# A two-layer hybrid DiT kernel: ScalarE's copies of the chunk inverses issued later, a seventh early spare block, and a third product bank in layer two

## The chip, the cores and the metric

One core of one Trainium2 chip runs the whole program. The metric is the device time of one execution in microseconds. The core has a matrix engine (PE, TensorE), a vector engine (DVE), a scalar engine (ACT), GpSimd (POOL) and a queue for transfers (SP); each issues its own instructions in the order in which the program gives them, and waits for the others by semaphores.

## What is computed

Two layers over 512 tokens of width 1024 with 256 context tokens beside them (768 columns in all; the second layer needs the context only as keys, values and starting states). Each layer projects the modulated, normalised input to three branches and to merge logits:

```python
h = rms_norm(x, norm_w[layer]) * (1.0 + scale) + shift
(a_qkv, a_z, a_beta, a_alpha, b_q, b_kv, b_z, c_qkv, c_z, merge) = split(h @ w_in[layer])
o_a = bidir_delta(conv+silu of a_qkv, ...)      # needs inv(L + I) of each 64x64 chunk
y_b = window_attention(q_b, k_b, v_b, k_ctx, v_ctx, sink) * silu(b_z)
o_c = bidir_retention(...)
merged = g_a * (y_a @ w_br[0]) + g_b * (y_b @ w_br[1]) + g_c * (y_c @ w_br[2])
x = x + gate * (merged @ w_o)
```

In branch A (gated delta rule) each chunk of 64 tokens needs the inverse of a unit lower-triangular matrix (`triangular_solve`), for four heads and two directions; queries, keys and values go through a five-tap convolution first. `g_a`, `g_b`, `g_c` are sigmoids of the merge logits, the gates `z` go through silu.

## The kernel before

Activations are kept transposed, 128 features by up to 768 tokens. A projection of one block of 128 outputs (`proj`, L322) takes float32 weights apart into a rounded high part `wh` (a copy on ACT, L306 through the helper L287) and a low part `wl` (four subtractions on POOL, L296), and the activations are held in the same two parts `hh` and `hl`. So one block is 24 matmuls of 512 columns on PE (`prod`, L311, all recorded at L261): 16 with `wh`, then 8 with `wl`. Where context is wanted, 24 more of 256 columns follow. The products go to PSUM tiles: `px` has two banks, `pc` one, `pg` five that serve everything else. The weight tiles `wr`, `wh` and `wl` have two buffers each.

Each layer first projects the blocks of branch A: `ak`, `aq` and `av` of each head. In `delta_proj` the result is convolved: ACT takes the first tap from `px` and `pc` (`t<-px,vec`, `t<-pc,vec`), DVE the other four taps (L290, `t<-px,vec,t` and `t<-pc,vec,t`), ACT applies a tanh, DVE a last L290 on the 768 columns, and PE turns the tile by transposes (L612, written to `pg`).

The inverses go through `delta_inv`: DVE solves the 32x32 corners lane by lane (31 steps, L293), then two stream transposes (L757, L758) bring the result back. It is then scattered to three sets of tiles: `W` by DVE (16 copies, L773), `T` and `Q` by ACT (12 copies of 32x192, L775; in the trace `t<-t 32x192` on ACT). `levels` builds the 64x64 inverses from these with many 32x32 matmuls (L801). `levels` is started by `burst`, which puts its first matmul in the PE order behind a given spare block.

A spare block is a projection whose result is needed only much later: the gates and merge logits, produced by the generator `aside` (L1224 on). Its product is evacuated by ACT with a tanh to a tile `kept` and stored to DRAM. Spare blocks are strewn between other work to keep PE busy; how many go where is the table `FILL` (L36), one row per layer: five numbers for the five weaves of branch A, one for each attention chunk, and one taken right before the token projection `w1` at the end of the attention. `aside` records for each spare block a triple in `self.asides`: the last matmul, an ACT instruction and the end. While `self.behind` is set (the first weave), each spare block is issued after the one before it. The first weave interleaves three generators by their counts:

```python
weave((seq(self.delta_mats(l, last, st[0]), self.delta_inv(st[0], BACK[l][0])), 45),
      (self.delta_proj(l, 1, vec, last, st[1]), 6), fill(F[0]))
```

The order in which the framework puts instructions on each engine follows from this program order, from priorities, and from `issue_after`, which orders one instruction behind another without a semaphore wait.

In the merge (end of `layer`), each of 24 products of 12 matmuls (`y` against `w_br`) goes to a `px` bank, and DVE multiplies it into the kept logits (L290, `t<-t,px`). The first of them run while DVE still normalises the last retention head (`c_norm`, L973 to L981).

Of the kernel before, what the change touches and what calls it, by code (L numbers as in the profile page):

```python
# [9 lines left out]
F32 = mybir.dt.float32  # L10
F32R = mybir.dt.float32r
BF16 = mybir.dt.bfloat16
AF = mybir.ActivationFunctionType
# [19 lines left out]
C1 = 3  # L33
AH = 2
BG = (0, 2)
FILL = ((5, 2, 4, 7, 6, 1, 0), (6, 2, 4, 9, 6, 1, 1))  # L36
BACK = ((2, 3), (2, 2))

NAMES = (["aq%d" % i for i in range(4)] + ["ak%d" % i for i in range(4)]
# [123 lines left out]
class Builder:  # L163
# [135 lines left out]
    def weight(self, dram, kb=KB):  # L299
        nc = self.nc  # L300
        w = self.wr.tile([128, KB, 128], F32, name="wr")[:, 0:kb]
        hi = self.wh.tile([128, KB, 128], F32R, name="wh")[:, 0:kb]
        lo = self.wl.tile([128, KB, 128], F32R, name="wl")[:, 0:kb]
        with self.tc.high_priority(offset=WHI):
            self.fetch = nc.sync.dma_start(w, dram).ins
            self.act(hi, w, AF.Copy)  # L306
            for k in range(0, kb, 2):
                self.gtt(lo[:, k:k + 2], w[:, k:k + 2], hi[:, k:k + 2].bitcast(F32), ALU.subtract)
        return [hi[:, k] for k in range(kb)], [lo[:, k] for k in range(kb)]
# [11 lines left out]

    def proj(self, dram, acts, ctx, w=None, other=False):  # L322
        w = w or self.weight(dram, len(acts))
        px = self.gps() if other else self.px.tile([128, 512], F32, name="px")
        self.prod(px, w, acts, slice(0, SEQ))
        pc = None
        if ctx:
            pc = self.gps(CTX) if other else self.pc.tile([128, 512], F32, name="pc")[:, 0:CTX]
            self.prod(pc, w, acts, slice(SEQ, TOK))
        return px, pc  # L330
# [396 lines left out]
    def delta_inv(self, st, back):  # L727
# [21 lines left out]
        for m in range(31):  # L749
            n, w = 31 - m, m + 1  # L750
# [14 lines left out]
        for d in range(2):  # L765
# [3 lines left out]
            for hh, h in enumerate(st.heads):  # L769
                W[h, d] = self.alloc()  # L770
                nc.gpsimd.memset(W[h, d].f, 0.0)
                for q in range(4):
                    made.append(nc.vector.tensor_copy(blk(W[h, d], q), lane(wsrc, q, d, hh)))  # L773
                for q, t, c in ((own, Q, 32 * (own % 2)), (own + 1 - 2 * d, Q, 32 * (1 - own % 2)), (other, T, 0)):
                    with self.tc.issue_after(self.asides[-back][1]):  # L775
                        made.append(self.act(six(t.f)[32 * q:32 * q + 32, hh, :, c:c + 32],
                                             lane(tsrc, q, d, hh), AF.Copy))
                yield
# [445 lines left out]
    def aside(self, l, last):  # L1224
# [5 lines left out]
        a, b = FILL[l][0], sum(FILL[l][0:4]) - 2  # L1230
        for nm in ms[0:a] + z("a")[0:2] + ms[a:b] + z("a")[2:4] + z("b") + z("c") + ms[b:]:
            px, pc = self.pblk(l, nm, not last, None, self.behind)
            pe = self.last
            t = self.fp.tile([128, TOK], F32, name="kept")
            for ps, sl in ((px, slice(0, SEQ)), (pc, slice(SEQ, TOK)))[:1 if last else 2]:
                th = self.act(t[:, sl], ps, AF.Tanh, scale=0.5)
                if nm[1] == "z":
                    self.stt(t[:, sl], t[:, sl], 1.0, ps, ALU.add, ALU.mult)
            self.asides.append((pe, th.ins, self.end))
            g = self.dp.tile([128, n], F32, name="%s_%d" % (nm, l))  # L1240
            nc.scalar.dma_start(g, t[:, 0:n])
            self.kept[nm] = g
# [10 lines left out]
    def layer(self, l, xs, rs, mod, vec, row, ada):  # L1253
# [9 lines left out]
        for k in range(KB):  # L1263
            self.tap("hh%d_%d" % (l, k), self.hs[k][0].f)
            self.tap("hl%d_%d" % (l, k), self.hs[k][1].f)
        self.asides, self.behind = [], False
        self.fill = self.aside(l, last)
        self.mods = self.ada(ada) if ada else iter(())
        F = FILL[l]
# [38 lines left out]
        for _ in p0:  # L1308
            pass
        self.behind = True  # L1310
        weave((seq(self.delta_mats(l, last, st[0]), self.delta_inv(st[0], BACK[l][0])), 45),
              (self.delta_proj(l, 1, vec, last, st[1]), 6), fill(F[0]))
        self.behind = False
        weave((self.hi(self.delta_chain(l, last, st[0])), 6), fill(F[1]))
        weave((self.hi(self.delta_mats(l, last, st[1])), 4), fill(F[2]))
# [195 lines left out]
```

## Time and profile before

| what | us |
|---|---|
| three executions | 1800.25, 1798.98, 1794.04 |
| median of them | 1798.98 |
| the profiled execution | 1798.01 |
| its span, first to last instruction | 1796.2 |
| PE busy in it | 1703.9 |
| mean granted TensorE clock | 0.982 |

The span is the time from the first to the last instruction of the profiled execution; 1.8 us lie around it. Times in the views are counted from the span's start. In a row of a timeline the first number is the start, the second the duration, `xN` the number of like instructions in a run, and the bracket the idle time of the engine before it with the instruction that ended it. Lines L261, L287, L290, L293 and L296 are those of small helpers (matmul, activation, the two vector operations and the POOL one), so the tile names tell which work it is.

### The profile page before, as it was taken

What the parts mean: (1) busy time and instruction counts of PE and PEld (TensorE: products, weight loads), DVE (VectorE), ACT (ScalarE), POOL (GpSimd) and SP (SyncE); (2) the same over time, 40 slices, a digit from 0 to 9 for tenths busy, and PEclk for the clock granted to TensorE, in tenths of its full rate; (3) what the DMA queues carried; (4) which work ended last, traced back from release to release, by engine and by line L of the source; (5) the groups of instructions that cost most, each with busy time, mean ns of one, the idle gap of its engine ahead of it and who ended that gap; (6) DMA issues with size and microseconds to landing.
All of it is one profiled execution on the core that took longest, in us unless ns stands there. A gap on an engine that the chain in (4) does not pass through costs nothing. (4 is left out here: it accounts for less than half of the span.)

```text
span 1796.2 us, 30682 instructions
## 1 busy us (share of the span) xinstructions
PE 1703.9 (95%) x11574; PEld 1449.5 (81%) x11574; DVE 1062.3 (59%) x2531; ACT 844.8 (47%) x2018; POOL 593.4 (33%) x739
## 2 busy tenths in 40 slices
PE   7899989999999999999999899969999999999997
PEld 4788879889877778988888687859878777888786
DVE  4668758634565464346573657966954667445663
ACT  6565546253454455233133556455554655433244
POOL 2422422412321313121454524433523323322453
PEclk9999999999999999999999999989999999999998
DMA  9202211313234234013444211211423432212552
GB/s 313 82 30 71 86 34 63 112 54 130 103 124 154 91 120 148 24 36 121 147 150 160 83 36 68 86 42 54 148 82 131 138 102 71 89 47 67 164 173 90
DMA packets 73748, 180.67 MB, mean 101 GB/s; under 512 B 8832, under 2 KB 16384, under 8 KB 73600
## 3 DMA queue, kind: packets, MB, share of 16 engines
q1 hardware_dynamic: 62144, 154.07, 26.3%
q10 hardware_dynamic: 11456, 24.65, 3.6%
q8 instruction: 91, 1.49, 0.3%
q14 instruction: 57, 0.47, 0.1%
HBM read 150.89 MB, written 27.79 MB: 99 GB/s over the span
## 5 line engine op out<-in xcount | busy, mean ns | idle before, releaser
L296 POOL TENSOR_TENSOR wl<-wr,wh 128x256 fp32r<-128x256 f32 x640 | 506.6, 821 | 1016.6 <-ACT wh L287 773.6
L261 PE MATMUL px<-hh,wh 128*128 128x512 f32 (+1 forms) x1000 | 392.9, 397 | 13.2 <-ACT wh L287 10.3
L261 PE MATMUL px<-hl,wh 128*128 128x512 f32 (+1 forms) x1000 | 392.3, 395 | 3.9 <-DVE hl L290 2.4
L293 DVE TENSOR_TENSOR t<-t,t 128x512 f32<-128x512 f32 (+21 forms) x411 | 264.3, 644 | 41.0 <-ACT t L287 28.5
L287 ACT ACTIVATE wh<-wr 128x1024 fp32r<-128x1024 f32 (+1 forms) x184 | 174.3, 947 | 220.9 <-PE pc L261 83.1
L261 PE MATMUL px<-hh,wl 128*128 128x512 f32 (+1 forms) x1000 | 262.1, 391 | 0.0
L287 ACT ACTIVATE t<-t 32x192 f32<-32x192 f32 (+10 forms) x314 | 167.4, 546 | 186.7 <-DVE t L290 144.9
L261 PE MATMUL pg<-t,t 128*128 128x128 f32 (+2 forms) x1616 | 230.9, 285 | 11.0 <-DVE t L293 10.6
L261 PEld LDWEIGHTS pg<-t,t 128*128 128x128 f32 x1616 | 205.8, 191 | 33.4 <-issue 11.2
L261 PEld LDWEIGHTS px<-hh,wh 128*128 128x128 f32 x1000 | 190.8, 191 | 52.0 <-ACT wh L287 11.2
L261 PEld LDWEIGHTS px<-hl,wh 128*128 128x128 f32 x1000 | 190.7, 191 | 40.4 <-DVE hl L290 5.7
L261 PEld LDWEIGHTS px<-hh,wl 128*128 128x128 f32 x1000 | 180.7, 189 | 33.2 <-issue 1.2
L261 PE MATMUL pc<-hl,wh 128*128 128x256 f32 x528 | 133.7, 288 | 0.9 <-DVE hl L290 0.8
L261 PE MATMUL pc<-hh,wh 128*128 128x256 f32 x528 | 133.4, 287 | 0.2 <-ACT hh L287 0.2
L287 ACT ACTIVATE t<-pg 128x128 f32<-128x128 f32 (+4 forms) x216 | 77.8, 384 | 108.9 <-PE pg L418 39.7
L261 PE MATMUL px<-t,wh 128*128 128x512 f32 x384 | 100.9, 400 | 4.5 <-DVE t L290 4.2
L261 PEld LDWEIGHTS pc<-hl,wh 128*128 128x128 f32 x528 | 101.2, 192 | 4.7 <-DVE hl L290 1.5
L261 PEld LDWEIGHTS pc<-hh,wh 128*128 128x128 f32 x528 | 101.1, 192 | 4.2 <-issue 1.2
L287 ACT ACTIVATE t<-px 128x128 f32<-128x128 f32 (+2 forms) x120 | 54.6, 465 | 91.2 <-PE px L261 85.3
L261 PE MATMUL px<-t,hh 128*128 128x272 f32 (+1 forms) x384 | 87.5, 316 | 0.3 <-DVE t L290 0.3
L261 PEld LDWEIGHTS px<-t,wh 128*128 128x128 f32 x384 | 71.2, 191 | 19.1 <-DVE t L290 3.1
L261 PE MATMUL pg<-hh,wh 128*128 128x256 f32 (+1 forms) x264 | 79.7, 326 | 3.0 <-DVE t L290 2.9
(192 smaller groups left out, 2657.3 us busy)
## 6 DMA issues: line engine op xcount, KB each, us to landing
wr<-wblk SPq DMA_DIRECT2D x120, 512.0 KB, 3.3
t<-wada SPq DMA_DIRECT2D x48, 384.0 KB, 4.6
wr<-wbr SPq DMA_DIRECT2D x48, 256.0 KB, 2.7
m<-kept ACTq DMA_DIRECT2D x24, 384.0 KB, 2.3
t<-m SPq DMA_DIRECT2D x24, 384.0 KB, 3.4
wr<-wout SPq DMA_DIRECT2D x16, 512.0 KB, 3.5
t<-wada SPq DMA_DIRECT2D x24, 256.0 KB, 4.8
m<-kept ACTq DMA_DIRECT2D x24, 256.0 KB, 2.0
```

The source lines that it names most:

```text
L261: return self.nc.tensor.matmul(out, lhsT=lhsT, rhs=rhs, start=start, stop=stop)
L287: return self.nc.scalar.activation(out, in_, func, **k)
L293: self.nc.vector.tensor_tensor(out=out, in0=in0, in1=in1, op=op)
L296: self.nc.gpsimd.tensor_tensor(out=out, in0=in0, in1=in1, op=op)
```

## The change

Three edits. In `delta_inv` the 12 ACT copies of `T` and `Q` are issued after the last spare block's ACT weight conversion (`self.high`, the copy to `wh`) instead of after the tanh of the spare block two or three back. In `FILL` layer two's first weave takes 7 spare blocks for 6 and none is left for the place before `w1`, and the first weave's count for `delta_proj` is 7 for 6 in both layers. In `proj` every third product of layer two that has no context part and isn't sent to `pg` uses the `pc` bank. After the change the lines from L321 on stand 3 or 4 lines lower (L612 is L615, L758 is L761, L801 is L804).

```diff
-FILL = ((5, 2, 4, 7, 6, 1, 0), (6, 2, 4, 9, 6, 1, 1))
+FILL = ((5, 2, 4, 7, 6, 1, 0), (7, 2, 4, 9, 6, 1, 0))
...
-            self.act(hi, w, AF.Copy)
+            self.high = self.act(hi, w, AF.Copy).ins
...
     def proj(self, dram, acts, ctx, w=None, other=False):
         w = w or self.weight(dram, len(acts))
-        px = self.gps() if other else self.px.tile([128, 512], F32, name="px")
+        self.turns += not (other or ctx)
+        third = self.three and not ctx and self.turns % 3 == 0
+        px = self.gps() if other else (self.pc if third else self.px).tile(
+            [128, 512], F32, name="pc" if third else "px")
...
-                    with self.tc.issue_after(self.asides[-back][1]):
+                    with self.tc.issue_after(self.asides[-1][1]):
...
-            pe = self.last
+            pe, high = self.last, self.high
...
-            self.asides.append((pe, th.ins, self.end))
+            self.asides.append((pe, high, self.end))
...
+        self.three, self.turns = last, 0
...
-              (self.delta_proj(l, 1, vec, last, st[1]), 6), fill(F[0]))
+              (self.delta_proj(l, 1, vec, last, st[1]), 7), fill(F[0]))
```

What moves on the engines, at three places.

PE in layer two's first weave, from the transposes of the last query head (`t608`) to the first matmul of `levels` (L801, L804). `t613` is the convolved last value head, `px_12384`, `pg_12084`, `pg_12074` and `pg_12124` are spare blocks. Before:

```order
L612 MATMUL pg_12030<-c0_108,t608_11856 128x128 x4
L261 MATMUL px_12384<-hh0_85,wh_12376 128x512
...
L261 MATMUL px_12384<-hh4_93,wl_12377 128x512
L612 MATMUL pg_12055<-c0_108,t613_11970 128x128 x4
L612 MATMUL pg_12061<-c0_108,t613_11970 128x128 x2
L261 MATMUL pg_12084<-hh0_85,wh_12076 128x512
...
L801 MATMUL pg_12155<-t619_12116,t572_11203 32x32
```

After:

```order
L615 MATMUL pg_12020<-c0_108,t608_11846 128x128 x4
L615 MATMUL pg_12045<-c0_108,t613_11960 128x128 x4
L615 MATMUL pg_12051<-c0_108,t613_11960 128x128 x2
L261 MATMUL pg_12074<-hh0_85,wh_12066 128x512
...
L261 MATMUL pg_12074<-hh7_99,wl_12067 128x512
L261 MATMUL pg_12124<-hh0_85,wh_12116 128x512
L804 MATMUL pg_12193<-t619_12154,t572_11203 32x32
```

The value head's transposes now stand right behind the query head's; before, 21 matmuls of a spare block stood between. Behind them stand 24 matmuls of one spare block and one of the next, where four matmuls stood; `levels` begins at the same place in the order.

ACT in layer one's first weave, the copies of `T` and `Q` (`32x6x32`), the first taps of the last value head (`t160`) and the conversion `wh_2624` of a spare block. Before:

```order
L287 ACTIVATE t163_2354<-t134_1540 32x6x32 x2
L287 ACTIVATE t163_2354<-t133_1539 32x6x32 x2
L287 ACTIVATE t156_2160<-t155_2149 128x768
...
L287 ACTIVATE wh_2624<-wr_2623 128x1024
...
L287 ACTIVATE t164_2355<-t134_1540 32x6x32 x4
L287 ACTIVATE t164_2355<-t133_1539 32x6x32 x4
L287 ACTIVATE t160_2317<-px_2251,vec0_163 128x512
L287 ACTIVATE wh_2837<-wr_2836 128x1024
L287 ACTIVATE t160_2317<-pc_2276,vec0_163 128x256
```

After:

```order
L287 ACTIVATE r2_2268<-r2_2268 128x12
...
L287 ACTIVATE t164_2355<-t134_1540 32x6x32 x2
L287 ACTIVATE t163_2354<-t134_1540 32x6x32
L287 ACTIVATE t164_2355<-t134_1540 32x6x32 x2
...
L287 ACTIVATE t164_2355<-t133_1539 32x6x32 x2
L287 ACTIVATE t163_2354<-t133_1539 32x6x32
L287 ACTIVATE t160_2243<-px_2177,vec0_163 128x512
L287 ACTIVATE wh_2624<-wr_2623 128x1024
L287 ACTIVATE t160_2243<-pc_2202,vec0_163 128x256
```

The twelve copies were in two lots of four and eight, the first of them ahead of the tanh of `t156` and of `wh_2624`; now all twelve stand in a row, ahead of the first tap of `t160` and of `wh_2624`. On PE the spare block that stood between the projections of the last key and the last query head (`ak3`, `aq3`; 48 matmuls, in `pg`) is gone from there, and `aq3` follows `ak3` at once; 25 matmuls of a spare block in `pg` now stand behind the value head's transposes.

DVE in layer two's merge: products of the merge (`px_16962` on) taken from their banks, between the steps of `c_norm` (L973 to L981 before, L976 to L984 after). Before:

```order
L290 SCALAR_TENSOR_TENSOR t872_16953<-t872_16953,px_16962 128x512
L974 BN_AGGR cmv_16869<-cst_16868 128x2
L290 SCALAR_TENSOR_TENSOR t873_16976<-t873_16976,px_16985 128x512
L981 TENSOR_SCALAR t831_16279<-t831_16279,cmv_16869,crs_16870 128x128 x4
...
L290 SCALAR_TENSOR_TENSOR t868_16921<-pg_16923,nw1_10485,t868_16921 128x512
...
L290 SCALAR_TENSOR_TENSOR t871_16945<-pg_16947,nw1_10485,t871_16945 128x512
L290 SCALAR_TENSOR_TENSOR t874_16999<-t874_16999,px_17008 128x512
L290 SCALAR_TENSOR_TENSOR t875_17022<-t875_17022,px_17031 128x512
```

After:

```order
L290 SCALAR_TENSOR_TENSOR t872_16953<-t872_16953,pc_16962 128x512
L977 BN_AGGR cmv_16869<-cst_16868 128x2
L290 SCALAR_TENSOR_TENSOR t873_16976<-t873_16976,px_16985 128x512
L290 SCALAR_TENSOR_TENSOR t874_16999<-t874_16999,px_17008 128x512
L984 TENSOR_SCALAR t831_16279<-t831_16279,cmv_16869,crs_16870 128x128 x4
...
L290 SCALAR_TENSOR_TENSOR t868_16921<-pg_16923,nw1_10485,t868_16921 128x512
...
L290 SCALAR_TENSOR_TENSOR t871_16945<-pg_16947,nw1_10485,t871_16945 128x512
L290 SCALAR_TENSOR_TENSOR t875_17022<-t875_17022,pc_17031 128x512
L290 SCALAR_TENSOR_TENSOR t876_17045<-t876_17045,px_17054 128x512
L290 SCALAR_TENSOR_TENSOR t877_17068<-t877_17068,px_17077 128x512
```

The third product (`px_17008`) is now taken ahead of the normalisation and the first (`pc_16962`) and fourth (`pc_17031`) lie in the third bank; on PE the product that alternates with the normalised tiles' transposes (L932) was the fourth and is the fifth.

## Rows read from the trace of the kernel before

**Rows 1.** The page, busy time by engine (share of the span, number of instructions).

```profile
PE 1703.9 (95%) x11574; PEld 1449.5 (81%) x11574; DVE 1062.3 (59%) x2531; ACT 844.8 (47%) x2018; POOL 593.4 (33%) x739
```

**Rows 2.** What PE waited for, whole span: us in total, times, longest us.

```profile
PE px L261 <- ACT wh L287: 10.6, 2, 10.3
...
PE pg L612 <- DVE t L290: 9.8, 5, 4.9
```

**Rows 3.** PE in time order, layer two's first weave: start, duration, [idle before <-releaser].

```profile
1179.23 0.63 PE L612 MATMUL pg<-c,t 128*128 128x128 f32 x4 [1.56 <-DVE t L290]
...
1190.20 0.80 PE L261 MATMUL px<-hh,wh 128*128 128x512 f32 x1 [10.34 <-ACT wh L287]
...
1196.89 0.82 PE L612 MATMUL pg<-c,t 128*128 128x128 f32 x6
...
1198.80 1.02 PE L801 MATMUL pg<-t,t 32*32 32x32 f32 x96 [0.16 <-DVE t L773]
```

**Rows 4.** ACT in time order, same stretch.

```profile
1181.90 3.22 ACT L287 ACTIVATE t<-t 32x192 f32<-32x192 f32 x6 [0.36 <-ACT r L287]
...
1189.10 1.06 ACT L287 ACTIVATE wh<-wr 128x1024 fp32r<-128x1024 f32 x1
...
1194.56 0.85 ACT L287 ACTIVATE t<-t 128x768 f32<-128x768 f32 x1 [3.01 <-DVE t L290]
```

**Rows 5.** DVE in time order, same stretch.

```profile
1181.04 4.47 DVE L773 COPY t<-t 32x192 f32<-32x192 f32 x8
...
1185.86 3.10 DVE L290 SCALAR_TENSOR_TENSOR t<-px,vec,t 128x510 f32<-128x510 f32 x4 [0.35 <-ACT t L287]
...
1190.55 1.00 DVE L290 SCALAR_TENSOR_TENSOR t<-pc,vec,t 128x254 f32<-128x254 f32 x2 [1.59 <-ACT t L287]
...
1195.59 0.96 DVE L290 SCALAR_TENSOR_TENSOR t<-t,t 128x768 f32<-128x768 f32 x1
```

**Rows 6.** Stretches: length, busy us of PE, PEld, DVE, ACT, POOL; clock, DMA.

```profile
1190.10:1193.60 3.50, 3.40 (x8) 2.73 (x9) 1.52 (x4) 1.45 (x10) 3.37 (x5) 0.50 0.00 0
...
1254.00:1316.40 62.40, 59.97 (x264) 49.00 (x262) 58.04 (x107) 33.30 (x69) 34.30 (x44) 1.00 0.41 140
...
1316.40:1321.00 4.60, 4.58 (x195) 3.77 (x199) 0.26 (x1) 2.03 (x3) 2.78 (x4) 0.56 0.18 64
...
1534.40:1548.30 13.90, 12.27 (x88) 9.79 (x86) 10.27 (x29) 10.39 (x31) 8.60 (x10) 1.00 0.51 164
```

**Rows 7.** PE in time order, layer one's first weave.

```profile
222.18 0.82 PE L612 MATMUL pg<-c,t 128*128 128x128 f32 x6
...
232.71 1.54 PE L612 MATMUL pg<-c,t 128*128 128x128 f32 x6 [4.90 <-DVE t L290]
...
235.46 1.50 PE L801 MATMUL pg<-t,t 32*32 32x32 f32 x96
```

**Rows 8.** ACT in time order, same stretch of layer one.

```profile
217.76 4.54 ACT L287 ACTIVATE t<-t 32x192 f32<-32x192 f32 x8 [0.30 <-ACT r L287]
...
222.33 0.69 ACT L287 ACTIVATE t<-px,vec 128x512 f32<-128x512 f32 x1
...
222.91 1.05 ACT L287 ACTIVATE wh<-wr 128x1024 fp32r<-128x1024 f32 x1
```

**Rows 9.** DVE in time order, same stretch of layer one.

```profile
206.02 3.06 DVE L290 SCALAR_TENSOR_TENSOR t<-px,vec,t 128x510 f32<-128x510 f32 x4
...
223.05 3.10 DVE L290 SCALAR_TENSOR_TENSOR t<-px,vec,t 128x510 f32<-128x510 f32 x4 [6.45 <-ACT t L287]
```

**Rows 10.** PE in time order, levels of layer two's second inverse.

```profile
1316.42 1.27 PE L801 MATMUL pg<-t,t 32*32 32x32 f32 x96 [2.45 <-ACT t L287]
```

**Rows 11.** PE in time order, layer two's merge.

```profile
1664.63 3.42 PE L261 MATMUL px<-t,wh 128*128 128x512 f32 x8 [2.75 <-DVE t L290]
...
1675.12 2.06 PE L261 MATMUL px<-t,wh 128*128 128x512 f32 x8 [1.31 <-DVE t L290]
```

**Rows 12.** DVE in time order, layer two's merge.

```profile
1666.58 5.17 DVE L981 TENSOR_SCALAR t<-t,cmv,crs 128x128 f32<-128x128 f32 x16 [1.33 <-ACT crs L287]
```

More of the change, by code (lines that the diff above doesn't have):

```diff
@@ L1232, in aside @@
             px, pc = self.pblk(l, nm, not last, None, self.behind)
-            pe = self.last
+            pe, high = self.last, self.high
             t = self.fp.tile([128, TOK], F32, name="kept")
             for ps, sl in ((px, slice(0, SEQ)), (pc, slice(SEQ, TOK)))[:1 if last else 2]:
-                th = self.act(t[:, sl], ps, AF.Tanh, scale=0.5)
+                self.act(t[:, sl], ps, AF.Tanh, scale=0.5)
                 if nm[1] == "z":
                     self.stt(t[:, sl], t[:, sl], 1.0, ps, ALU.add, ALU.mult)
-            self.asides.append((pe, th.ins, self.end))
+            self.asides.append((pe, high, self.end))
             g = self.dp.tile([128, n], F32, name="%s_%d" % (nm, l))
```

## The prediction

> **What bounds the kernel now.** I read the busy row first: PE works 1703.9 us of 1796.2, so the time is PE's work plus PE's holes, and no edit here removes a matmul [rows 1]. So I went on to the list of what PE waited for. The edit about `wh` aims at one hole of 10.3 us; transposes (L612) waiting for DVE lose 9.8 us in five holes [rows 2]. Then came the timelines around both, and the stretches with their granted clock. In layer two's first weave the reader is to see PE stop at 1179.9 after four transposes, start again at 1190.20 with the conversion `wh` that ACT began at 1189.10, turn the last value head at 1196.89 and reach `levels` at 1198.80 [rows 3, 4]. A hole costs more than its length: the eight matmuls after this one took 3.40 us at a granted clock of 0.50, the 1.2 GHz level, where one takes 0.227 us at full clock (59.97 us for 264), so 3.40 - 1.8 = 1.6 us more [rows 6]. The sum below is made against the profiled execution, 1798.01 us, 1.0 under the median 1798.98. A measurement of this kernel can tell about 0.3% or 5.4 us from no change.
>
> **Copies and seventh spare block, layer two's first weave.** The wait for `wh` goes: the spare block that waited no longer stands there. But the value head's transposes now come right behind the query head's, and everything that could fill the hole stands behind them. So I work out when they can run, along DVE, whose order stays the same. The second stream transpose ends at 1181.0; eight copies of 4.47 us follow, to 1185.5; four taps on `px` take 3.10, to 1188.6 (before, they began at 1185.86 after waiting 0.35 for ACT's first tap, so little is gained) [rows 5]. The taps on `pc` waited 1.59 us for ACT, which had twelve copies in two lots of 3.22 us and the conversion of 1.06 ahead of its tap [rows 4, 5]; now that tap is early, and the four taps, two small instructions and a copy take about 2.3 us: 1190.9. ACT's tanh is 0.85, with three DVE copies of 1.07 us beside it, and the last vector step 0.96: 1193.0 against 1196.55 before [rows 4, 5]. So PE idles from 1179.9 to 1193.0, 13.1 us instead of 10.34; after it come 0.6 us of transposes and 25 matmuls of 5.7 us plus 1.6 for the clock: `levels` at 1200.9 against 1198.80 [rows 3, 6]. As many matmuls are done by then as before, so this is **+2 us**. Bounds: -1 (transposes ready at 1190) and +4 (the copies on ACT get in front of the tanh, 0.54 us each).
>
> **The same in layer one.** Here 48 matmuls leave the place between `ak3` and `aq3`, so `aq3` has to wait for the single `pc` bank (about 1.8 us, what DVE needs for the four `pc` taps), and the value head's product ends near 215.3 instead of 222.18 [rows 7]. The inverses come later, since `aq3`'s taps (about 5.5 us; the first four take 3.06) now precede the stream transposes that ended at 206.02: 211.5 [rows 9]. The twelve copies follow behind a table load on ACT, from about 213.2; at 4.54/8 = 0.57 us each they end at 220.0. Behind them wait the tap (0.69) and the conversion (1.05) of the spare block that PE wants next: 221.7 [rows 8]. PE has finished its transposes at about 216.1, so it idles 5.6 us. After 21 matmuls, 4.8 us plus 1.6 for the clock, it is 228.1; the value head is ready 9.6 us after its taps begin, as before (223.05 to 232.7): 230.3 [rows 7, 9]. So another 2.2 us, transposes, 25 matmuls: `levels` near 236.5 against 235.46, with 3.4 us less work done (23 matmuls on `pc`, three on `px`). Against this stands the hole of 4.90 us that goes, already in these times. **+4 us**; bounds +1 (the copies begin at 210) and +6 (they begin where the eight did, at 217.76).
>
> **Layer two's second inverse.** `levels` waits 2.45 us for the last ACT copy, and the clock falls to 0.56 for the next 4.6 us [rows 6, 10]. By the order 17 more spare matmuls now stand ahead of it, 17 x 0.227 = 3.9 us, which is more than the hole even with a conversion of 1.05 us ahead of the copies. **-2.5 us**; bounds -3.3 (the clock stays up as well) and 0 (the copies slide along).
>
> **The spare matmuls have to be missing somewhere**: at the end of layer two's attention. `FILL`'s last number drops to 0, and by the order the last chunk has 1.5 matmuls of 512 columns to fill with instead of 21. That chunk took 13.9 us with 12.27 of PE, 10.27 of DVE and 10.39 of ACT [rows 6]. With 19.5 x 0.227 = 4.4 us taken away PE has 7.9, and ACT and DVE set the pace at 10.4 plus about 1.1 of waits between them: 11.5 - 7.9 = 3.6 us of idle instead of 1.6. I take **+2.5**, since the weights of the token projection are then late too; bounds 0 and +4.4 (the chunk keeps its length).
>
> **The third bank.** In the merge PE waits 2.75 us for a `px` bank, runs eight matmuls in 3.42 us after it, and waits 1.31 us for another [rows 11]. Now the third product finds a free bank and DVE takes it ahead of the normalisation; the one that alternates with the transposes is the fifth. What is late next: the 16 steps at L981, which ACT releases at 1666.58 and which end at 1671.75 [rows 12]; the last transpose can't run sooner. With five matmuls behind it PE has finished the fifth product at 1673.1. Before, this product began at 1675.12 and took 12 x 0.227 = 2.7: 1677.8. **-4.7**, of which I take -4.4; bounds -5.7 (both holes and the 1.6 us) and 0. The Trainium skill says, on the page "Perfetto Trace Analysis" in the section "Matmuls", that independent matmul groups should rotate through different banks so that the evacuation of one overlaps the next; by that alone the whole 5.7 us would go. The rows put the normalisation in the way of about 1 us of it. Elsewhere in layer two the first copy out of a `px` is mostly ahead of PE: nothing. Layer one's second inverse only has its copies overtake one evacuation, on an engine that isn't the last there: nothing, 0.4 us either way.
>
> **Sum**: +2 + 4 - 2.5 + 2.5 - 4.4 = +1.6, so 1798.0 + 1.6 = **1799.6 us**, no change that can be told.
>
> **Rivals.**
> (a) Faster: the holes that the edits aim at go and the cover is not missed. For it speaks that in layer two PE only needs the value head a little earlier and that in layer one four copies ran right behind the stream transposes, before ACT's eight [rows 8]; against it, that all twelve now stand in one row ahead of a conversion. It would be 0 in both first weaves, -2.5, +1 at the attention, -5.7: -7.2, 1790.8.
> (b) Slower: layer one's conversion behind the twelve copies. If they start where the eight started, at 217.76, the spare block's `wh` is there at 226.3 and PE idles 10 us before it; the value head then is ready at 234.9, and `levels` comes 4.6 us later than I say. With layer two's end at its bound (+4.4) this is 1.6 + 4.6 + 1.9 = +8, 1806. It decides from a start of the copies after about 216. For it speaks that ACT was late with just these copies before [rows 8]; against it, that the evacuations that delayed it now stand elsewhere.
> (c) The bank rule in full: both merge holes vanish, 5.7 us instead of 4.4: 1798.3, still no change. The page named above would have it so.
> (d) The order moves, but other work closes ranks everywhere: 1798.
>
> **How the numbers follow.** Forecast 0.35, (c) 0.10, (d) 0.08: together no change 0.53. (a) 0.22, (b) 0.25, a little more than (a) since each of the two weaves has a new wait in a row. The predicted time is that of the forecast. The range takes in (a) and (b) and leaves about one in ten out on each side: 1791 to 1808.
>
> **What would show it.** Right: in layer two one hole of about 13 us on PE ahead of the L615 transposes, ended by DVE, and none ended by `wh`; in layer one a new hole of about 5 us at 221, ended by the conversion `wh`, and a shorter one ahead of the transposes than 4.90; no hole at the second inverse's `levels`; idle of over 3 us in the last attention chunk; no wait of 2.75 us in the merge, and a wait for L984 in its place. Wrong: a hole in layer two under 9 us, no hole for `wh` in layer one, or merge holes of the same sum as before.

## The result and the profile after

| | median us | from, to |
|---|---|---|
| the kernel before (4 runs on the same chip) | 1799.37 | 1794.04, 1800.25 |
| the changed kernel (4 runs) | 1808.18 | 1807.53, 1810.05 |

The ratio is 1.0051, with a 95% interval of 1.0036 to 1.0066: the change costs about 9 us, where 1799.6 was forecast. The profiled execution of the changed kernel took 1808.64 us, its span is 1806.8, 10.6 more than before. The page's busy row shows that PE has the same number of matmuls as in [rows 1]; 6.8 us of the loss are PE busy for longer, at a mean granted clock of 0.977 for 0.982, the rest are holes.

```profile
PE 1710.7 (95%) x11574; PEld 1455.0 (81%) x11574; DVE 1062.8 (59%) x2531; ACT 845.4 (47%) x2018; POOL 595.6 (33%) x739
```

To see where the 10.6 us arise I counted PE's matmuls in both traces and subtracted the start of the n-th before from that of the n-th after. Inside a place whose order changed this difference means little; behind it, it is what the place cost in this one profile; how far that can be trusted stands in the last section. The forecast's terms stand beside.

| place (difference behind it at matmul) | cost, us | forecast |
|---|---|---|
| start, nothing of the change in it (900) | +1.4 | 0 |
| layer one, first weave (2100) | +2.6 | +4 |
| layer one, second inverse (3300) | +1.9 | 0 |
| layer one's merge (6000) | -0.8 | 0 |
| layer two, first weave (8400) | +5.1 | +2 |
| layer two, second inverse and attention end (10500) | +1.8 | -2.5 + 2.5 |
| retention (10800) | +0.6 | 0 |
| third bank in the merge (11100) | -3.4 | -4.4 |
| tail (end of the span) | +1.4 | 0 |

**Layer two's first weave.** PE in time order, which answers to [rows 3] (start, duration, idle before and what ended it): the hole for `wh` is gone and the one ahead of the value head's transposes is 15.24 us, not the 13.1 of the forecast.

```profile
1185.21 0.63 PE L615 MATMUL pg<-c,t 128*128 128x128 f32 x4 [2.43 <-DVE t L290]
1201.07 1.54 PE L615 MATMUL pg<-c,t 128*128 128x128 f32 x6 [15.24 <-DVE t L290]
...
1210.05 1.02 PE L804 MATMUL pg<-t,t 32*32 32x32 f32 x96
```

DVE in time order there, which answers to [rows 5]. The order is the one forecast and the taps on `px` take their 3.10 us as before, but the eight copies take 6.84 us for 4.47.

```profile
1185.14 1.95 DVE L761 STREAM_TRANSPOSE t<-t 128x1024 f32<-128x1024 f32 x1
1187.01 6.84 DVE L776 COPY t<-t 32x192 f32<-32x192 f32 x8
1193.88 3.10 DVE L290 SCALAR_TENSOR_TENSOR t<-px,vec,t 128x510 f32<-128x510 f32 x4
1196.90 0.99 DVE L290 SCALAR_TENSOR_TENSOR t<-pc,vec,t 128x254 f32<-128x254 f32 x2
```

ACT beside it, which answers to [rows 4]: `wh` is converted at 1188.40, while DVE copies; in the kernel before it was converted after them.

```profile
1188.40 1.05 ACT L287 ACTIVATE wh<-wr 128x1024 fp32r<-128x1024 f32 x1
...
1191.24 3.75 ACT L287 ACTIVATE t<-t 32x192 f32<-32x192 f32 x7
```

POOL, whose four subtractions `wl` are released by `wh`: it is busy from 1187.15 to 1193.74, for nearly as long as DVE copies.

```profile
1187.15 1.02 POOL L737 MEMSET t<- 128x1024 f32 x1 [0.61 <-DVE t L761]
...
1188.31 1.64 POOL L296 TENSOR_TENSOR t<-t,r 128x768 f32<-128x768 f32 x1
1189.92 3.14 POOL L296 TENSOR_TENSOR wl<-wr,wh 128x256 fp32r<-128x256 f32 x4
1193.01 0.73 POOL L774 MEMSET t<- 128x768 f32 x1
```

**Layer one's first weave**, PE, which answers to [rows 7]: the three holes forecast are there, 1.63 us for `pc`, 2.89 for `wh` and 0.82 for the transposes in place of 4.90.

```profile
196.75 0.35 PE L261 MATMUL pc<-hh,wh 128*128 128x256 f32 x1 [1.63 <-DVE t L290]
...
220.75 0.79 PE L261 MATMUL px<-hh,wh 128*128 128x512 f32 x1 [2.89 <-ACT wh L287]
...
229.43 0.88 PE L615 MATMUL pg<-c,t 128*128 128x128 f32 x6 [0.82 <-DVE t L290]
```

ACT there, to [rows 8]: the twelve copies begin at 212.31 and the conversion follows them.

```profile
212.31 6.73 ACT L287 ACTIVATE t<-t 32x192 f32<-32x192 f32 x12 [2.26 <-POOL t L765]
...
219.65 1.05 ACT L287 ACTIVATE wh<-wr 128x1024 fp32r<-128x1024 f32 x1
```

**Layer one's second inverse**, PE: `levels` stops for 2.19 us; the same stop was 1.71 us before, and the 82 matmuls behind it took 2.17 us there instead of 3.48 for 81. Before, then after:

```profile
372.47 2.17 PE L801 MATMUL pg<-t,t 32*32 32x32 f32 x82 [1.71 <-issue]
```

```profile
376.62 3.48 PE L804 MATMUL pg<-t,t 32*32 32x32 f32 x81 [2.19 <-issue]
```

**The end of layer two's attention**, PE: waits for DVE and ACT that weren't covered any more, and a fall of the clock (0.68 granted in the stretch from 1546 to 1562, where the last chunk had 1.00 in [rows 6]). PE is busy for 12.37 of these 16.00 us, so it idles 3.6; the forecast had said over 3.

```profile
1550.65 0.97 PE L1155 MATMUL pg<-c,t 128*128 128x128 f32 x5 [1.16 <-DVE t L1147]
1552.31 2.54 PE L1155 MATMUL pg<-c,t 128*128 128x128 f32 x10 [0.69 <-DVE t L1147]
1555.68 3.68 PE L1166 MATMUL pg<-t,t 128*64 128x256 f32 x16 [0.83 <-ACT t L287]
```

**The merge**, to [rows 11]: the waits of 2.75 and 1.31 us for `px` are gone; PE waits for the normalised tiles (L984) instead.

```profile
1680.85 0.58 PE L935 MATMUL pg<-c,t 128*128 128x128 f32 x2 [0.84 <-DVE t L984]
...
1683.42 0.33 PE L935 MATMUL pg<-c,t 128*128 128x128 f32 x1 [0.41 <-DVE t L984]
```

### The profile page after: what moved, and what is told of

The parts are those of the page before. It is cut to its first block, busy times and chain, and to the rows that moved or that the text cites. A ratio compares the mean times of both kernels' runs of the same rounds, so it can differ in the third digit from the quotient of the medians.

```text
span 1806.8 us, 30679 instructions
## 1 busy us (share of the span) xinstructions
PE 1710.7 (95%) x11574; PEld 1455.0 (81%) x11574; DVE 1062.8 (59%) x2531; ACT 845.4 (47%) x2018; POOL 595.6 (33%) x739
## 5 line engine op out<-in xcount | busy, mean ns | idle before, releaser
L261 PE MATMUL px<-hh,wh 128*128 128x512 f32 (+1 forms) x888 | 348.5, 397 | 6.1 <-ACT wh L287 3.1
L261 PE MATMUL px<-hl,wh 128*128 128x512 f32 (+1 forms) x888 | 348.7, 396 | 3.3 <-DVE hl L290 1.8
L261 PE MATMUL px<-hh,wl 128*128 128x512 f32 (+1 forms) x888 | 230.8, 390 | 0.0
L261 PEld LDWEIGHTS px<-hh,wh 128*128 128x128 f32 x888 | 169.7, 192 | 40.3 <-ACT hh L287 5.2
L261 PEld LDWEIGHTS px<-hl,wh 128*128 128x128 f32 x888 | 170.6, 192 | 36.3 <-DVE hl L290 4.8
L261 PEld LDWEIGHTS px<-hh,wl 128*128 128x128 f32 x888 | 160.5, 190 | 29.2 <-issue 0.8
L261 PE MATMUL pc<-hl,wh 128*128 128x256 f32 (+1 forms) x632 | 174.6, 305 | 0.9 <-DVE hl L290 0.8
L261 PE MATMUL pc<-hh,wh 128*128 128x256 f32 (+1 forms) x632 | 173.7, 304 | 1.7 <-DVE t L290 1.6
L261 PE MATMUL pc<-hh,wl 128*128 128x256 f32 (+1 forms) x632 | 106.2, 304 | 0.0
L261 PEld LDWEIGHTS pc<-hh,wl 128*128 128x128 f32 x632 | 87.9, 191 | 4.6 <-issue 1.2
```

The lines of the kernel that those rows point to most:

```text
L261: return self.nc.tensor.matmul(out, lhsT=lhsT, rhs=rhs, start=start, stop=stop)
```

## The experiments

Times are medians, ratios are to the kernel before on the same chip, with the 95% interval. Ratios are compared, not medians, where two kernels ran on different chips. The expectations call the edits "copies" (ScalarE's copies of the inverses), "pace" (7 for 6) and "third bank". The seventh spare block, the fourth part of the change, was neither run alone nor taken out alone: what it does shows only together with the pace.

### One edit alone

The third bank alone in the kernel before:

```diff
+        self.turns += not (other or ctx)
+        third = self.three and not ctx and self.turns % 3 == 0
+        px = self.gps() if other else (self.pc if third else self.px).tile(
...
+        self.three, self.turns = last, 0
```

> The kernel before with the third product bank alone. Theory (the parts add up as the aligned traces of before and after say): PE reaches the end of the merge 3.4 us earlier (12.51 to 9.11 us behind), nothing else moves, so about 1796 against 1799.4 (-3.4). Rival (the bank only moves the wait, and the 1.5 us by which the changed kernel's end is later belongs to it): -2 or less, 1797.5 and up. The hole of 2.75 us ahead of the third product must be gone in both; the waits for L984 (0.84 and 0.41 us in the changed kernel) come in its place.

Measured 1795.97 us, 0.9978 (0.9966 to 0.9989): a gain of 4 us, and the merge gained 2.7 by the count of matmuls. The theory was right; of the three edits tried alone it is the one that pays. One wait of 1.37 us for a `px` bank stays in this kernel, where the changed kernel has none.

The copies alone:

```diff
-                    with self.tc.issue_after(self.asides[-back][1]):
+                    with self.tc.issue_after(self.asides[-1][1]):
...
-            self.asides.append((pe, th.ins, self.end))
+            self.asides.append((pe, high, self.end))
```

> The kernel before with the copies of T and Q behind the last spare block's conversion, alone; PE's order is that of before. Theory (a wait put in the place of another): in layer two the conversion comes some 7 us earlier, so PE takes its 21 matmuls early, but the value head's transposes become the next wait; POOL's subtractions for that weight then run beside DVE's copies and stretch them, as in the changed kernel (eight copies 6.84 us for 4.47). Sum of the holes there 8 to 10 us for 10.34, levels 0 to 2 us earlier; in layer one the twelve copies in a row start near 217.8 and push the last value head back by 2.3 us: together +-1 us, 1799 to 1801. Rival (the edit does what it says, a wait for wh of 10.3 us goes): 1790 to 1793.

Measured 1808.09 us, 1.0044 (1.0028 to 1.006): a loss of 8 us, and a miss of every theory. In the first weaves nothing moved: PE still waits 10.35 us for `wh` in layer two and 4.87 for the transposes in layer one, and the order of every engine there is that of the kernel before. The loss is in the second inverses: +2.5 us in layer one, where PE's order isn't quite that of before either, and +7.3 in layer two (at matmul 8700; 5.1 are left of it at the attention's end). PE and ACT in layer two, in time order:

```profile
1319.10 0.80 PE L261 MATMUL px<-hh,wh 128*128 128x512 f32 x1 [8.07 <-ACT kept L287]
```

```profile
1312.52 5.91 ACT L287 ACTIVATE t<-t 32x192 f32<-32x192 f32 x12 [7.59 <-DVE t L758]
1318.45 0.60 ACT L287 ACTIVATE kept<-px 128x512 f32<-128x512 f32 x1
```

The twelve copies stand at the head of ACT's queue before their data are there. ACT idles 7.59 us for DVE's stream transpose, then copies for 5.91, and only then empties the `px` bank for which PE waits 8.07 us. Before, the copies stood behind an evacuation, and their data were nearly there:

```profile
1308.57 0.60 ACT L287 ACTIVATE kept<-px 128x512 f32<-128x512 f32 x1 [0.70 <-PE px L261]
1310.20 3.87 ACT L287 ACTIVATE t<-t 32x192 f32<-32x192 f32 x7 [1.03 <-DVE t L758]
```

The pace alone, `delta_proj`'s count 7 for 6:

> The kernel before with 7 for 6 in the weave, alone; PE's order in layer one becomes that of the changed kernel, in layer two it stays. Theory: layer one's loss belongs to this number: the projection of the last query head waits 1.6 us for the one bank, levels come no earlier with 3.4 us less work done, and the second inverse is 1.9 us slower: +3 to +5 us, 1802 to 1804. Rival (the loss is that of the twelve copies in a row ahead of the conversion, which are not in this kernel): 0 to +1.5 us, 1799 to 1801, and no hole ended by the conversion wh near 221.

Measured 1803.35 us, 1.0022 (1.0009 to 1.0035), as the theory said. PE in layer one:

```profile
197.57 0.36 PE L261 MATMUL pc<-hh,wh 128*128 128x256 f32 x1 [2.04 <-DVE t L290]
...
221.56 0.50 PE L261 MATMUL px<-hh,wh 128*128 128x512 f32 x1 [2.86 <-ACT wh L287]
...
230.21 1.54 PE L612 MATMUL pg<-c,t 128*128 128x128 f32 x6 [3.56 <-DVE t L290]
```

The holes of layer one come with the pace, not with the copies: the twelve copies stand in a row here too. The weave costs 4.2 us by the count of matmuls. One part of the theory fails: the second inverse isn't slower here (-0.1 us), so its loss belongs to the copies.

### One edit taken out of the changed kernel

Without the third bank (`px` always from its own two banks):

> The changed kernel without the third bank. Theory (two effects of that bank): the merge gives back 3 to 4 us, and in layer two's second inverse ACT's twelve copies, which wait for DVE's stream transpose, hold up the evacuation behind them, so that PE runs out of px banks as with the copies alone (a hole of 8.07 us there); the seventh block's matmuls don't help against a full bank. So +3.5 and +4 to +8 against the changed kernel: 1815 to 1820. Rival (the bank counts in the merge alone, and the further spare matmuls fill the inverse): 1811 to 1813, no hole over 3 us between 1310 and 1330.

Measured 1.0096 (1.0081 to 1.0111), 0.0045 or 8 us above the changed kernel. The merge's two waits are back, 3.4 us by the count of matmuls:

```profile
1684.41 3.46 PE L261 MATMUL px<-t,wh 128*128 128x512 f32 x8 [2.76 <-DVE t L290]
...
1694.91 2.08 PE L261 MATMUL px<-t,wh 128*128 128x512 f32 x8 [1.58 <-DVE t L290]
```

The second inverse in layer two has a hole of 0.78 us only, the rival's sign; some 1.5 us are lost across it against the changed kernel (matmuls 8100 to 9300). Another 5.2 us were lost in layer one, where the order of the work is that of the changed kernel: 3.6 in the first weave, where this profile is the slowest and the changed kernel's the fastest of seven with that order, and 1.6 in the second inverse, at a granted clock of 0.90 for 0.95 from 365 to 400. So the size came out, but the place of its second half did not.

Without the copies (issued after the tanh of the block two or three back, as before):

> The changed kernel with the copies of T and Q placed as before (behind the tanh of the spare block two back). Theory (the copies edit costs in the second inverses, and is needed only where the sixth block stands behind the transposes): layer one's second inverse about 2 us better; in layer two's first weave the copies now wait for the sixth block's tanh, levels come 3 to 4 us later with 23 more spare matmuls (5.2 us of work) done: -1 to -2 us. Sum 1804 to 1806. Rival (the copies edit is what keeps the changed kernel from being worse): 1809 or more.

Measured 1.0075 (1.0062 to 1.0088), 0.0024 or 4 us above the changed kernel; the ends of the two intervals overlap. The rival was right: together with the pace, layer two's first weave needs the copies early. Its `levels` waits for them behind a conversion:

```profile
1201.99 1.54 PE L615 MATMUL pg<-c,t 128*128 128x128 f32 x6 [15.22 <-DVE t L290]
...
1219.36 1.02 PE L804 MATMUL pg<-t,t 32*32 32x32 f32 x96 [2.71 <-ACT t L287]
```

The run also shows that the hole of 15 us isn't the work of the copies edit. It is here without that edit, and DVE's eight copies are as slow as in the changed kernel:

```profile
1187.94 6.81 DVE L776 COPY t<-t 32x192 f32<-32x192 f32 x8
```

With the pace alone the hole is the old one, 10.35 us for `wh`, and the copies take 4.45 us; with seven blocks at the pace of 6 (the next run) they take 4.36. So it takes the pace and the seventh block together.

Without the pace (6, with seven spare blocks left in layer two):

> The changed kernel with 6 instead of 7 in the weave: layer one's first weave as before, and layer two's seventh block stands between the last key head and the value head, ahead of the query head's transposes, followed by 21 matmuls ahead of the value head's transposes as before. Theory (it is the place of the spare blocks behind the transposes that loses, not their number): layer one gains 3 to 4 us; in layer two the hole ahead of the 21 matmuls is 10.3 less nothing, since ACT's copies and conversion keep their order, but levels come with 24 more matmuls done and PE reaches the hole 5.5 us later: hole 4 to 5 us, 6 us saved against the changed kernel's 15.24 and 2.43; the attention still lacks its block. Sum 1797 to 1800. Rival (the extra block pushes DVE's solve back by as much, because its projection comes later): hole stays near 10, 1802 to 1805.

Measured 1.004 (1.0027 to 1.0054), a miss: no gain that the intervals can tell. By the count of matmuls layer one's first weave is 3.4 us cheaper than in the changed kernel, as it should be, and layer two's 2.2, with several waits in place of the one long hole. The second inverses take it back: 1.9 us more in layer one's, where the stop inside `levels` is 3.42 us for 2.19, and 4.2 more from layer two's to the attention's end. ACT's copies wait 7.78 us for DVE there, and `levels` waits for them. PE, first in layer two's first weave, then in its second inverse:

```profile
1179.52 1.54 PE L615 MATMUL pg<-c,t 128*128 128x128 f32 x6 [3.69 <-DVE t L290]
...
1200.52 0.50 PE L261 MATMUL px<-hh,wh 128*128 128x512 f32 x1 [3.49 <-ACT wh L287]
...
1327.91 1.49 PE L804 MATMUL pg<-t,t 32*32 32x32 f32 x96 [2.47 <-ACT t L287]
...
1333.47 2.51 PE L804 MATMUL pg<-t,t 32*32 32x32 f32 x130 [1.76 <-ACT t L287]
```

The copies edit only in the first weaves, in the changed kernel (`th` is the tanh of the spare block):

```diff
-                    with self.tc.issue_after(self.asides[-1][1]):
+                    with self.tc.issue_after(self.asides[-1][1] if self.behind else self.asides[-back][3]):
...
-            self.asides.append((pe, high, self.end))
+            self.asides.append((pe, high, self.end, th.ins))
```

> The changed kernel with the copies edit kept in the first weaves and taken back in the second inverses. Theory (in a second inverse the twelve copies wait for DVE's stream transpose at the head of ACT's queue and hold up the evacuation of px behind them; the copies alone cost 2.5 us in layer one's and 7.3 us in layer two's second inverse): layer one's second inverse 1.5 to 2 us better; in layer two's the third bank and the 17 matmuls have hidden most of it, 0 to 1.5 us better. Sum -1.5 to -3.5 against the changed kernel: 1804.5 to 1806.5. Rival (those costs are the phase of the clock, not the queue): 1807.5 or more.

Measured 1806.4 us, 1.0033 (1.0022 to 1.0044): 0.0018 or 3 us below the changed kernel, which the two intervals can't tell from nothing. The place can: layer one's second inverse is 2.2 us shorter by the count of matmuls, and the stop inside `levels` is 1.36 us.

### Why eight copies took 6.84 us

The same eight values written by another operation, to tell a slow copy from a slow read:

```diff
-                    made.append(nc.vector.tensor_copy(blk(W[h, d], q), lane(wsrc, q, d, hh)))
+                    made.append(nc.vector.scalar_tensor_tensor(out=blk(W[h, d], q), in0=lane(wsrc, q, d, hh), scalar=1.0,
+                                                               in1=lane(wsrc, q, d, hh), op0=ALU.mult, op1=ALU.max))
```

> The changed kernel with DVE's 16 copies of W in each inverse written as a two-operand instruction (scalar_tensor_tensor, maximum of x and x) that gives the same values; PE's order is that of the changed kernel. Theory (DVE's plain copies are held up by POOL's instructions beside them: in the changed kernel they end when those end, 0.75 to 1.5 us each instead of 0.32): each of the 16 takes about 0.32 us whatever POOL does, the eight of layer two 2.6 us for 6.84, and the hole of 15.24 us shrinks to about 11; layer one gains about 1 us as well: -4 to -6 us against the changed kernel, 1802 to 1804. Rival (it isn't the kind of instruction but a shared memory or the order of the queue): the new instructions are stretched too, no gain over 1 us, 1807 to 1809.

Measured 1.005 (1.003 to 1.0069), no gain, with a hole of 16.21 us; the theory that only the plain copy is held up fell. DVE, single instructions of the eight, and POOL beside them:

```profile
1189.55 0.51 DVE L776 SCALAR_TENSOR_TENSOR t<-t 32x192 f32<-32x192 f32 x1
...
1192.29 0.94 DVE L776 SCALAR_TENSOR_TENSOR t<-t 32x192 f32<-32x192 f32 x1
```

```profile
1189.21 0.95 POOL L737 MEMSET t<- 128x1024 f32 x1 [0.62 <-DVE t L761]
...
1191.89 2.89 POOL L296 TENSOR_TENSOR wl<-wr,wh 128x256 fp32r<-128x256 f32 x3
```

Beside the memset, which reads nothing, the new form takes its own 0.51 us; beside the subtraction `wl`, which reads, 0.94.

POOL's `wl` of that spare block held back until DVE's eighth copy is done:

```diff
+                    if self.three and self.behind and (d, hh, q) == (0, 1, 3):
+                        for i in self.late:
+                            self.tc.add_manual_dep(i, made[-1].ins.name, mybir.DependencyInfo(
+                                mybir.DependencyClass.Sync, mybir.DependencyReason.DATA), reason="late")
```

> The changed kernel with one wait added: in layer two's first weave POOL's four subtractions for the seventh block start only after DVE's eighth copy of W (the order of every engine stays). Theory (these subtractions, run at the same time, are what stretches DVE's copies): the last four copies take 0.3 us each again instead of 0.75 to 1.37, the eight together 4.5 us instead of 6.84, and the value head's transposes start 2 to 2.4 us earlier in that stretch (hole 12.8 to 13.3 for 15.24): -2 us, about 1806. Rival (the copies are slow for ACT's copies beside them, or because of their own addresses): still 6.5 us or more, 1808.

PE, DVE (the eight, then the seventh of them alone) and POOL:

```profile
1202.85 1.54 PE L617 MATMUL pg<-c,t 128*128 128x128 f32 x6 [12.86 <-DVE t L290]
```

```profile
1191.15 4.47 DVE L778 COPY t<-t 32x192 f32<-32x192 f32 x8
1194.63 0.32 DVE L778 COPY t<-t 32x192 f32<-32x192 f32 x1
```

```profile
1195.85 2.78 POOL L296 TENSOR_TENSOR wl<-wr,wh 128x256 fp32r<-128x256 f32 x4 [1.75 <-DVE t L778]
```

The taps on `px`, which now run beside `wl`, keep their 3.10 us. The copies are back at 4.47 us, the hole at 12.86, close to the 13.1 of the forecast, and the weave costs 3.0 us less by the count of matmuls. The total is unchanged (1.0049, 1.0036 to 1.0061): this run lost 4.7 us more than the changed kernel's before it came to that weave, 2.5 of it in layer one's second inverse, where with the same order the stop inside `levels` is 3.77 us for 2.19 and the granted clock from 365 to 400 is 0.90 for 0.95. The place shows the cause; the total doesn't show the gain.

### A version that beats both

In the kernel before, ACT's twelve copies of the first weaves only ordered behind the last value head's first taps (no pace, no seventh block):

```diff
-            self.act(acc.f[:, base:base + n], ps[:, 0:n], AF.Copy, scale=taps[:, 2:3])
+            self.first = self.act(acc.f[:, base:base + n], ps[:, 0:n], AF.Copy, scale=taps[:, 2:3]).ins
...
+        for c in st[0].copies:
+            self.tc.add_manual_dep(c, self.first.name, info, reason="tap")
```

> The kernel before, and in the first weaves the twelve copies are issued behind the first taps of the last value head (t<-px,vec and t<-pc,vec); the spare block's conversion wh then comes ahead of them too, and PE's order is nearly that of before. Theory (what was missing in the change is cover ahead of the value head's transposes, and an early tap): layer one's hole of 4.90 us shrinks by 2 to 3 us; in layer two the 21 matmuls run inside the hole of 10.34 us, which becomes 3 to 5 us for wh and 3 to 6 us for the transposes (POOL's subtractions beside DVE's copies take back 2.4 us): levels 1 to 3 us earlier. Sum -3 to -6: 1793.5 to 1796.5. Rival (levels then wait for the copies on ACT instead, which end only some 4 us after the tanh): +-1, 1798.5 to 1800.5, with holes ended by ACT t at L801.

Measured 1796.44 us, 0.9981 (0.9969 to 0.9993). In layer two the holes came as the theory said, 3.66 us for `wh` and 4.45 for the transposes, with DVE's eight copies at 6.90 us. In layer one the hole of 4.90 is 2.89, but `levels` then waits 2.04 us for DVE's copies. The count of matmuls finds little of the gain in this run's own profile: 0.4 and 0.2 us in the two first weaves, 1.1 from layer two's second inverse to the attention's end. With the third bank:

> As the run before, with the third bank as well. Theory (they touch different stages, so their gains add; the third bank alone gave -4.0): -7 to -10 against before, 1789.5 to 1792.5. Rival (no sum): 1794 to 1796.

Measured 1793.2 us, 0.9959 (0.9943 to 0.9974), just above the theory's range; by the ratios the two gains of 0.0022 and 0.0019 add. With `wl` held back as well:

> As the run before, and in layer two's first weave POOL's subtractions for the spare block whose weight now comes early wait for DVE's eighth copy of W. Theory (POOL beside DVE's copies stretches them by 2.4 us, as it did in the changed kernel): eight copies 4.5 us, transposes 2 us earlier, a further -1 to -2.4 us: 1788 to 1791. Rival (the 21 matmuls end with those that need wl, and PE now waits for them): no gain or up to 1 us lost, a hole ahead of matmuls with wl.

Measured 1791.84 us, 0.9952 (0.9938 to 0.9967), 8.5 us below the kernel before and about 1% below the changed one. Over the version ahead of it the intervals can't tell a gain, which leaves the theory unproven in the total; the place shows it, with DVE's eight copies at 4.53 us for 6.91 and the weave 4.2 us cheaper by the count of matmuls. DVE and PE in layer two's first weave, where 10.34 us were lost in one hole [rows 3]:

```profile
1182.51 4.53 DVE L779 COPY t<-t 32x192 f32<-32x192 f32 x8
```

```profile
1185.02 0.79 PE L261 MATMUL px<-hh,wh 128*128 128x512 f32 x1 [3.66 <-ACT wh L287]
...
1194.30 0.88 PE L617 MATMUL pg<-c,t 128*128 128x128 f32 x6 [1.95 <-DVE t L290]
```

The spare block still stands between the two transposes and still covers; only what ran ahead of its conversion has moved.

## Why the prediction was wrong

The forecast was no change, the result a loss of 0.5%, just outside the range. By its own steps:

- **Layer two's first weave, +2, measured +5.1** (5.3 and 5.6 in two further profiles with the same order on PE). The chain was right: no wait for `wh`, one hole ended by DVE, and DVE's order sets its length. The step that failed is "eight copies of 4.47 us follow". That sum of [rows 5] already held two copies of 0.99 and 1.51 us beside POOL's work and six of some 0.32 alone; the early conversion brings `wl`, and the memset behind it, beside the last four, and they take 0.75 to 1.37 us. I costed what the early conversion does for PE and not what it sets going on POOL. Nor is it the copies edit that brings the conversion early, as I had it: without that edit the hole is 15.22 us too. Shown by the run with `wl` held back: 4.47 us and a hole of 12.86. This is 2.1 of the 3.1 us; the other 1.0 stands behind the hole, where the transposes and 25 matmuls up to `levels` take 9.0 us for the 7.9 of the sum.
- **Layer one's first weave, +4, measured +2.6.** Right in mechanism, and in size too: this profile is the lowest of seven with PE's order there, the others 3.2 to 6.2, their middle 4.0 (4.2 with the pace alone). The holes are of the kind that was forecast: a wait for `pc` of 1.63 us (1.8 forecast), one for `wh`, a shorter one for the transposes. The hole for `wh` is 2.89 and not 5.6, since the copies began at 212.31, a little sooner, and PE came later than reckoned.
- **Layer one's second inverse, "nothing, 0.4 us either way", measured +1.9.** This step failed. In the six profiles with the copies edit there, PE's stop inside `levels` is 2.19 to 3.77 us and the place costs 1.9 to 4.4; in the eight without it the stop is 1.20 to 1.71 and the place costs -0.3 to 0.8. The run with the edit kept to the first weaves wins it back. The sum let the copies overtake one evacuation and left PE as it was, but in these six PE's own order differs there too (81 matmuls behind the stop for 82). What ends the stop the profile doesn't say ("issue"), so why it is longer stays open.
- **Layer two's second inverse and the attention's end, -2.5 + 2.5, measured +1.8 together.** There is no hole at `levels`, as forecast, and waits on DVE and ACT at the attention's end. How the sum splits I can't show, because the spare matmuls that moved lie between; nor is the +1.8 firm, since two other profiles with the same order on PE from there on (the other kind of copy, and `wl` held back) have 0.0 and -0.4. That the copies alone cost 7.3 us here was in no theory: I moved them on ACT and asked what waits behind a conversion, not what waits behind a copy that isn't ready. In the changed kernel the pace covers most of this (without it `levels` waits 2.47 and 1.76 us for the copies) and the third bank a part (without it PE waits 0.78 us for `px`).
- **The third bank, -4.4, measured -3.4**, 2.7 alone. Right in kind: the normalisation ends last, and PE waits for L984 as said. Rival (c), 5.7 us, is out. The rule of the Trainium skill that was named beside it (page "Perfetto Trace Analysis", section "Matmuls") agrees in that both waits for a bank are gone; the time by it, 5.7 us, doesn't come, because the normalisation is late next.
- **Start and tail, 0, measured +1.4 and +1.4.** Not shown to be of the change: the kernel with the third bank alone, whose order at the start is that of before, had +1.9 and +2.6 there, and that with the pace alone +1.8 and -0.5.

Without start and tail 7.8 us remain; the forecast had 1.6. The largest parts of the difference are layer two's first weave (3.1 us) and layer one's second inverse (1.9). Rival (b) named the right sign and nearly the time (1806), by luck: the conversion late in layer one, on which it rested, did not happen so. (a) fell.

The terms taken one edit at a time: third bank -4.0, pace +3.4, copies +8.1 us by medians, 7.5 in sum, where these three and the seventh block together cost 8.8. That is near by chance, for the parts don't add: the 8.07 us hole of the copies alone is covered in the changed kernel, and the hole of 15 us stands only where the pace and the seventh block come together.

## What to carry to other kernels

Before an instruction is moved up, ask two things: what stands behind it on its own queue if its data are late (here an evacuation, for 8.07 us), and which engine its result sets going, beside what (here POOL beside DVE's copies). Take the time of an instruction in a new neighbourhood from single rows that have the same neighbour, not from the mean of a mixed row. Where one late instruction makes a hole, move what delays it and leave the cover in place: the kernel that did only that is 0.2% faster, while moving the cover made a larger hole.

## What the runs showed of the hardware

**DVE's copies in SBUF stop for POOL.** A copy of 32x192 takes 0.32 us alone. Beside a POOL instruction that began before it, it ends 0.1 to 0.2 us behind that one: 0.99 us beside a memset of 1.02, 1.51 beside a subtraction of 1.64, 0.75 beside one of 0.81. Single rows of the changed kernel, DVE and then POOL:

```profile
1188.63 1.51 DVE L776 COPY t<-t 32x192 f32<-32x192 f32 x1
1190.16 0.75 DVE L776 COPY t<-t 32x192 f32<-32x192 f32 x1
```

```profile
1189.92 0.81 POOL L296 TENSOR_TENSOR wl<-wr,wh 128x256 fp32r<-128x256 f32 x1
```

The taps that read PSUM keep their 3.10 us for four in every run. The Trainium skill, page "SBUF — State Buffer", section "Who interferes with whom", says that DVE and GpSimd share a pair of SBUF ports: a copy can enter a two-port mode that uses the shared pair, and then the engine that issues first holds the pair for its whole instruction while the other is blocked; an instruction with two SBUF inputs collides only with a GpSimd instruction that reads; one with a single SBUF input, outside the two-port modes, not at all. The traces agree in all three: the copy 0.99 us beside a memset of 1.02 and 0.32 alone, the two-input form 0.51 beside a memset and 0.94 beside a subtraction, the taps 3.10 us for four beside `wl` too. That the copies were in a two-port mode no view shows.

**One profile tells a place's cost to some 2 us either way, and the granted clock is part of that.** Between 365 and 400 us the granted clock is 1.00 or 0.95 in the eight profiles without the copies edit in layer one's second inverse, 0.95 or 0.90 in the six with it; it differs between kernels with the same order there, too (0.95 in the changed kernel, 0.90 in the one with `wl` held back). Each step of 0.05 is 35 x 0.05 = 1.75 us of full clock, an estimate of what it costs a PE that is busy all the time. The seven profiles with one order on PE in layer one's first weave cost 2.6 to 6.2 us there. With the pace alone layer two's first weave, where its order is that of before, came out at +2.1. So a place's cost is shown where several profiles agree or where a hole and its releaser stand in the rows, and not by one difference.
